# Differential-attention logits as pairs of 64-row products in the two row halves of the TensorE array

## The chip, the cores and the metric

One core of a Trainium2 chip runs the whole program. The metric is the device time of one execution in microseconds (us), median of several runs. TensorE does the matmuls, VectorE and ScalarE the elementwise work, GpSimd a few memsets and loads, and SyncE's queue issues nearly all DMAs.

## What is computed

A trunk of two layers over 512 tokens of 1024 channels. Each layer has two SwiGLU blocks, a mixer and a gated per-layer embedding; the mixer of the first layer is attention, with a sparse group of 8 heads (top-k selected keys) beside a differential group of 4 heads. The change is in the differential group. Each of its heads has two maps of 64 channels, a softmax for each, and the difference of the two acts on values of 128 channels:

```python
def diff_attention(q, k, v, lam, subln_g, lam_init):
    """q, k (B,S,H,2,HD) with the two maps on axis 3; v (B,S,H,2HD)."""
    ...
        mask = key_chunk[None, :] <= q_chunk[:, None]
        s = jnp.einsum('bqhcd,bshcd->cbhqs', qb, k).astype(jnp.float32) * scale
        prob = jax.nn.softmax(jnp.where(mask, s, -jnp.inf), axis=-1)
        a = (prob[0] - lam * prob[1]).astype(v.dtype)
        return jnp.einsum('bhqs,bshe->bqhe', a, v)
```

Queries come in blocks of 128, and block t sees the first 128(t+1) keys.

## The kernel before

**Tiling.** Activations lie transposed, channels on the 128 partitions and the 512 tokens along the free axis. `SLOTS` fixes how many buffers of each kind there are: 28 of kind "a" (128x512, floats), 12 of kind "t", 8 PSUM tiles "ps" of 128x512. A large projection is a series of `mm3` (L278 to L284): three matmuls on values split in two parts (L281, L282, L283). A plain fp32 product is `mm` (L268 to L276); in the trace each of them is two instructions on TensorE, and each instruction has its own weight load (engine PEld).

**Order of the work.** No order is written out by hand. Each helper call appends an operation with a price in ns to `Plan`; `order()` (L140) then simulates the engines and always places the operation that can start first, the lower `prio` (place in the program plus a bias for its stream) where several can. What comes out is the fixed order of each engine's queue. The price of a plain product is in `mm`, L273: 1.68 ns a column, and L274 and L275 double it for operands of at most 64 partitions; no plain product of the kernel has such operands. Operations belong to streams, and `CAPS` (L1233) limits what a stream may hold: the logits of the differential group, stream "lgpvB", may hold 2 PSUM tiles and 6 "t" tiles at a time.

**The differential group.** `even_mixer` (L773) projects queries and keys of the 4 heads into 8 tiles `bqk`, each with the two maps of a head one above the other on the partitions (64 rows each). For the keys (L936 to L945) `halves()` (L828) takes two tiles of kind "a" and sets the half that is not the map's own to zero on GpSimd; the normalised key tile is then copied half by half into them by DMA (L944). So each map has a key tile of 128 rows, half of them zero, and the product of the full query tile with it is the map's logits. `softmax_exp_` (L953) does, for each map in turn, the product (L960) and VectorE's pass that adds the mask and takes the maximum (L962); then ScalarE's exponentials (L968) with their sums. The loop of stream "pvB" (L988 to L1013) goes over 4 heads and 4 query blocks: logits, the difference of the maps, transposes, and the product with the values `bv`. `softmax_exp_` also serves the sparse group (L1034), with keys stacked to 128 rows.

**Around it.** In the same stretch TensorE has the projections for the sparse group's queries (stream "aq", L974), the embedding products (`ple_proj`, L972) and, behind the group's last head, the output projection `down` (L1027). VectorE has the 48 rounds of the top-k selection (L904 to L917) at low priority.

Of the kernel before, what the change touches and what calls it, by code (L numbers as in the profile page):

```python
# [45 lines left out]
class View:  # L46
# [19 lines left out]
    def ap(self):  # L66
        x = self.store.real
        for name, args in self.steps:
            x = getattr(x, name)(*args)
        return x  # L70
# [187 lines left out]
def trunk(ctx: ExitStack, tc: tile.TileContext, A: dict, out: bass.AP):  # L258
# [9 lines left out]
    def mm(p, a, b, start, stop):  # L268
        n = b.n
        if a.store.dt == F32R:  # L270
            cost = max(213.0 if n < 256 and n < 192 else 0.0, n * 0.422)
        else:
            cost = 150.0 if a.n <= 64 and n <= 128 else max(n, 127) * 1.68  # L273
            if a.arr.shape[0] <= 64:  # L274
                cost *= 2  # L275
        P.op("PE", cost, lambda: nc.tensor.matmul(ap(p), ap(a), ap(b), start=start, stop=stop), w=[p], r=[a, b], lat=160.0)  # L276

    def mm3(p, a, b, first, last):  # L278
# [32 lines left out]
    def dve(o, fn, r, per=1.04, extra=(), fixed=0.0):  # L311
        P.op("DVE", per * o.n + 67.0 + fixed, fn, w=[o] + list(extra), r=r)

    def tmul(o, a, b):
        dve(o, lambda: nc.vector.tensor_mul(ap(o), ap(a), ap(b)), [a, b])  # L315
# [7 lines left out]
    def ts(o, a, s1, s2, op0, op1=None):  # L323
        kw = {} if op1 is None else {"op1": op1}
        dve(o, lambda: nc.vector.tensor_scalar(ap(o), ap(a), ap(s1), ap(s2), op0=op0, **kw), [a, s1, s2],
            per=1.04 if a.psum else 0.52, fixed=62.0 * (isinstance(s1, View) or isinstance(s2, View)))

    def stt(o, a, s, b, op0, op1, accum=None):
        kw = (lambda: {"accum_out": ap(accum)}) if accum is not None else dict
        dve(o, lambda: nc.vector.scalar_tensor_tensor(ap(o), ap(a), ap(s), ap(b), op0=op0, op1=op1, **kw()), [a, s, b],  # L330
            extra=[accum] if accum is not None else [], fixed=62.0 * isinstance(s, View))
# [4 lines left out]
    def recip(o, a):  # L336
        dve(o, lambda: nc.vector.reciprocal(ap(o), ap(a)), [a], per=6.3)
# [4 lines left out]
    def gset(o, x):  # L342
        P.op("POOL", 200.0 + 0.5 * o.n, lambda: nc.gpsimd.memset(ap(o), x), w=[o])

    def dma(o, x, kb, after=None):
        P.op("SP", max(500.0, kb * 2.7), lambda: nc.sync.dma_start(ap(o), ap(x)), w=[o], r=[x, after],
             lat=2000.0 if isinstance(x, View) and isinstance(o, View) else 2000.0)
# [4 lines left out]
    def ps(shape=(128, S)):  # L352
        return P.tile("ps", shape)
# [4 lines left out]
    def at(dt=F32, shape=(128, S)):  # L358
        return P.tile("a", shape, dt)

    def tt(dt=F32, shape=(128, S)):
        return P.tile("t", shape, dt)

    def small(*n):
        return P.tile("s", (128,) + n)
# [88 lines left out]
    for part in (GAINS[:1], GAINS[1:]):  # L454
# [7 lines left out]
        with P.on("norm", 60 * (len(gcol) - 1)):  # L462
            p = ps()
# [309 lines left out]
    def even_mixer(norm, nxt, cos, sin):  # L773
# [30 lines left out]
        def head_factor(c, R):  # L804
            v, f = small(NT, R), small(NT, R)
            for t in range(NT):
                ts(v[:, t, :], c[:, t, :], rc2[:, t:t + 1], EPS, OP.mult, OP.add)
            r = rsqrt(v.flat(), NT * R)
            for t in range(NT):
                ts(f[:, t, :], r[:, R * t:R * t + R], rcol[:, t, :], None, OP.mult)  # L810
            return f
# [13 lines left out]
                        dma(d[c][0].bitcast(F32)[half, :], (hi, lo)[b].bitcast(F32)[own, :], 128)  # L825
            return d

        def halves():  # L828
            d = [at(), at()]
            gset(d[0][64:128, :], 0.0)  # L830
            gset(d[1][0:64, :], 0.0)
            return d

        wv = w.rearrange("(k p) c -> p k c", p=128)

        def values(grp):
# [22 lines left out]
        with P.on("side", SIDE_BIAS):  # L859
# [12 lines left out]
            for t in range(NT):  # L872
                p = ps()
# [11 lines left out]
        with P.on("sc", SC_BIAS):  # L885

            score = [None]
            for t in range(1, NT):
                N = 128 * (t + 1)
                sc = at()  # L890
                for h in range(4):
                    p = ps()
# [11 lines left out]
        with P.on("topk", TOPK_BIAS):  # L904

            selb = [cmask[:, S - 128:S]]
            for t in range(1, NT):
                N = 128 * (t + 1)
# [13 lines left out]
        bqk = []  # L922
        for g in range(2):
            for j in range(2):
                u = wunit(w, 0, KD, 1028 + 512 * g + 256 * j, 256)
                for s in range(2):
                    i = 4 * g + 2 * j + s
                    p = ps()
# [5 lines left out]
        with P.on("side", SIDE_BIAS):  # L934
            fB = head_factor(rows, 16)
            fq = small(NT, 8)  # L936
            ts(fq, fB[:, :, 0:8], 0.125, None, OP.mult)
            bk = []
            for h in range(4):
                fb = bcast2(fB, 8 + 2 * h)  # L940
                d = halves()
                tmul(bqk[4 + h], fb, bqk[4 + h])
                for b in range(2):
                    dma(d[b][64 * b:64 * b + 64, :], bqk[4 + h][64 * b:64 * b + 64, :], 128)  # L944
                bk.append(d)  # L945

        P.stream = "main"

        def softmax_exp(*a):
            with P.on("lg" + P.stream, LG_BIAS if P.stream == "pvB" else LGA_BIAS):  # L950
                return softmax_exp_(*a)

        def softmax_exp_(maps, N, bias, fcol):  # L953
            n = len(maps)
            mx, nb, sm = small(n), small(n), small(n)
            es = []
            for i, (q, ks) in enumerate(maps):
                p = ps()
                for j, k in enumerate(ks):
                    mm(p[:, 0:k.n], q, k, j == 0, j == len(ks) - 1)  # L960
                e = tt()
                dve(e[:, 0:N], lambda e=e, p=p, i=i: nc.vector.tensor_tensor_reduce(  # L962
                    out=ap(e[:, 0:N]), in0=ap(p[:, 0:N]), in1=ap(bias), scale=1.0, scalar=LOW,
                    op0=OP.add, op1=OP.max, accum_out=ap(mx[:, i:i + 1])), [p, bias], extra=[mx])
                es.append(e)
            stt(nb, mx, -1.0, fcol, OP.mult, OP.mult)
            for i, e in enumerate(es):
                act(e[:, 0:N], e[:, 0:N], AF.Exp, scale=fcol[:, i:i + 1], bias=nb[:, i:i + 1], accum=sm[:, i:i + 1])  # L968
            recip(sm, sm)
            return es, sm  # L970
# [3 lines left out]
        with P.on("aq", AQ_BIAS):  # L974
# [3 lines left out]
            for j in range(2):  # L978
                u = wunit(w, 0, KD, 256 * j, 256)
                for s in range(2):  # L980
                    i = 2 * j + s
                    p = ps()
# [5 lines left out]
        with P.on("pvB"):  # L988
            c = ps((128, NT, 4))
            oc = []  # L990
            for h in range(4):
                po = ps()
                for t in range(NT):
                    N = 128 * (t + 1)
                    (e0, e1), rs = softmax_exp([(bqk[h][:, 128 * t:128 * t + 128], (bk[h][c][:, 0:N],)) for c in range(2)],
                                               N, cmask[:, S - N:S], fq[:, t, 2 * h:2 * h + 2])
                    tmul(rs[:, 1:2], rs[:, 1:2], nlam)
                    scaled(e1[:, 0:N], e1[:, 0:N], rs[:, 1:2])
                    stt(e0[:, 0:N], e0[:, 0:N], rs[:, 0:1], e1[:, 0:N], OP.mult, OP.add)
                    pT = ps()  # L1000
                    for b in range(t + 1):
                        transpose(pT[:, 128 * b:128 * b + 128], e0[:, 128 * b:128 * b + 128], ident)
                    aT = tt()
                    moved(aT[:, 0:N], pT[:, 0:N])
                    for b in range(t + 1):
                        mm(po[:, 128 * t:128 * t + 128], bv[b][:, 128 * h:128 * h + 128],
                           aT[:, 128 * b:128 * b + 128], b == 0, b == t)
                o = at()
                ts(o, po, 2.0 ** 80, -2.0 ** 80, OP.min, OP.max)
                sq = tt()  # L1010
                act(sq, o, AF.Square, scale=2.0 ** -30)
                colsums(c[:, :, h:h + 1], sq, ones[:, 0:1])
                oc.append(o)  # L1013
            v, ok, fo = small(NT, 4), small(NT, 4), small(NT, 4)
            ts(ok, c, 2.0 ** 68, None, OP.is_lt)
            ts(v, c, 2.0 ** 68 * (1.0 - 2.0 ** -24), 2.0 ** 53, OP.min, OP.mult)
            ts(v, v, EPS, None, OP.add)
            r = rsqrt(v.flat(), NT * 4, 2.0 ** -40)
            tmul(fo.flat(), r, ok.flat())
            bcats = []  # L1020
            for h in range(4):
                fb = bcast(fo[:, :, h:h + 1])
                stt(oc[h], oc[h], vcol[:, 8:9], fb, OP.mult, OP.mult)
                bcats.append(split(oc[h], at))
# [5 lines left out]
        for t in range(NT):  # L1030
            N = 128 * (t + 1)
            pa = ps()
            for h in range(0, 8, 2):
                es, rs = softmax_exp([(aq[h + c][:, 128 * t:128 * t + 128], [k[:, 0:max(N, 256)] for k in ak]) for c in range(2)],  # L1034
                                     N, selb[t], fA[:, t, h:h + 2])
# [15 lines left out]
    def bcast2(f, c0):  # L1051
        p = ps()
        w = tt(shape=(128, NT, 2, 64))
        vcopy(w, f[:, :, c0:c0 + 2][:, :, :, None].to_broadcast([128, NT, 2, 64]))
        for t in range(NT):
            transpose(p[:, 128 * t:128 * t + 128], w[:, t, :, :].flat(), ident)
        return p
# [133 lines left out]
    for k in range(KD):  # L1191
        with P.on("start"):
            p = ps()
# [76 lines left out]
```

## Time and profile before

| | |
|---|---|
| median of 3 runs | 2010.78 us (2010.63 to 2011.23) |
| profiled execution | 2010.54 us |
| its span, first to last instruction | 2008.6 us |
| TensorE busy | 1991.3 us (99%) |
| weight loads busy | 1630.2 us (81%) |
| VectorE busy | 1080.8 us (54%) |
| ScalarE busy | 723.2 us (36%) |
| logits of the differential group | 490.7 to 538 us |

In the profile PE is TensorE's matmuls, PEld its weight loads, DVE VectorE, ACT ScalarE, POOL GpSimd, SPq SyncE's queue. A matmul's duration holds the time that it takes to flow through the array, so what one costs in a row of many is read from the distance of the starts. A matmul that could follow at once may be recorded as starting while the one ahead still runs.

### The profile page before, as it was taken

How to read it: one execution, taken by the hardware profiler on the slowest of the kernel's cores; microseconds unless marked ns; L12 is line 12 of the kernel's file. 1: busy time of each engine (PE TensorE's matmuls, PEld its weight loads, DVE VectorE, ACT ScalarE, POOL GpSimd, SP SyncE). 2: the span in 40 equal slices, each digit the busy share in tenths (PEclk: the TensorE clock that was granted, in tenths of full speed). 3: DMA queues.
4: the chain of work that ended last, by engine and by line, in shares of the span. 5: the costliest groups of instructions: out<-in, count | busy, mean ns of one | idle time of the engine just before them, and what ended most of it. 6: DMA issues, size and time to landing. Idle time of an engine off the chain costs nothing.

```text
span 2008.6 us, 22735 instructions
## 1 busy us (share of the span) xinstructions
PE 1991.3 (99%) x9154; PEld 1630.2 (81%) x9154; DVE 1080.8 (54%) x1797; ACT 723.2 (36%) x1057; POOL 13.8 (1%) x35
## 2 busy tenths in 40 slices
PE   8999999999999999999999999999999999999999
PEld 7888888888767888888888888888767888888887
DVE  6442464489986544344466443444699744334443
ACT  6322233344756422132254222223425533213232
POOL 0000000000000000000000000000000000000000
PEclk9999999999999999999999999999999999999999
DMA  5323322354330323332233322323333232323222
GB/s 189 105 97 98 108 85 84 94 160 141 96 110 22 104 86 105 94 95 95 95 121 110 105 98 92 105 75 103 107 105 105 84 97 92 105 85 104 95 104 75
DMA packets 164778, 202.28 MB, mean 101 GB/s; under 512 B 9968, under 2 KB 123072, under 8 KB 164672
## 3 DMA queue, kind: packets, MB, share of 16 engines
q1 hardware_dynamic: 164016, 200.38, 31.3%
q8 instruction: 72, 1.18, 0.2%
q0 software_dynamic: 528, 0.41, 0.2%
q14 instruction: 34, 0.28, 0.0%
q10 hardware_dynamic: 128, 0.03, 0.0%
HBM read 185.33 MB, written 6.29 MB: 95 GB/s over the span
## 4 chain that ended last, share of the span: by engine, by line
PE 97%; DVE 1%; ACT 1%; DMA 1%; issue 0%; SPq 0%; ACTq 0%; DVEq 0%
PE ps L281 30%; PE ps L282 30%; PE ps L283 30%; PE ps L276 6%; PE ps L287 1%; DMA whi<-in_x_dram 0%; ACT t L292 0%; ACT t L297 0%; DVE t L962 0%; DVE t L330 0%; DVE wlo L330 0%; DMA t<-t 0%; DVE t L309 0%; DVE wlo L321 0%; DVE a L913 0%
## 5 line engine op out<-in xcount | busy, mean ns | idle before, releaser
L297 ACT CAST whi<-raw 128x1024 fp32r<-128x1024 f32 (+2 forms) x342 | 348.7, 1022 | 976.3 <-PE ps L282 936.7
L321 DVE TENSOR_TENSOR wlo<-raw,whi 128x1024 fp32r<-128x1024 f32 (+2 forms) x342 | 405.1, 1185 | 496.8 <-ACT whi L297 496.0
L281 PE MATMUL ps<-x,whi 128*128 128x512 f32 x1664 | 655.8, 394 | 0.6 <-ACT x L297 0.6
L282 PE MATMUL ps<-x,whi 128*128 128x512 f32 x1664 | 648.7, 390 | 0.6 <-DVE x L321 0.6
L283 PE MATMUL ps<-x,wlo 128*128 128x512 f32 x1664 | 648.8, 390 | 0.0
L281 PEld LDWEIGHTS ps<-x,whi 128*128 128x128 f32 x1664 | 313.1, 188 | 66.2 <-ACT x L297 1.1
L283 PEld LDWEIGHTS ps<-x,wlo 128*128 128x128 f32 x1664 | 312.9, 188 | 65.6
L282 PEld LDWEIGHTS ps<-x,whi 128*128 128x128 f32 x1664 | 313.2, 188 | 65.1 <-DVE x L321 1.2
L281 PE MATMUL ps<-a,whi 128*128 128x512 f32 x832 | 325.1, 391 | 0.0
L282 PE MATMUL ps<-a,whi 128*128 128x512 f32 x832 | 323.9, 389 | 0.0
L283 PE MATMUL ps<-a,wlo 128*128 128x512 f32 x832 | 323.8, 389 | 0.0
L281 PEld LDWEIGHTS ps<-a,whi 128*128 128x128 f32 x832 | 156.3, 188 | 32.8 <-issue 0.5
L283 PEld LDWEIGHTS ps<-a,wlo 128*128 128x128 f32 x832 | 156.2, 188 | 32.6
L282 PEld LDWEIGHTS ps<-a,whi 128*128 128x128 f32 x832 | 156.2, 188 | 32.3 <-DVE a L321 0.7
L315 DVE TENSOR_TENSOR t<-ps,t 128x512 f32<-128x512 f32 x88 | 60.8, 691 | 209.1 <-PE ps L283 208.3
L315 DVE TENSOR_TENSOR t<-ps,rb 128x512 f32<-128x512 f32 x100 | 68.7, 687 | 112.1 <-PE ps L283 109.9
L330 DVE SCALAR_TENSOR_TENSOR a<-a 128x508 f32<-128x508 f32 (+23 forms) x108 | 72.7, 731 | 5.0 <-ACT a L292 4.6
L292 ACT ACTIVATE t<-t 128x512 f32<-128x512 f32 x100 | 62.9, 629 | 22.9 <-DVE t L315 22.8
L297 ACT CAST a<-t 128x512 fp32r<-128x512 f32 x88 | 54.8, 623 | 36.8 <-DVE t L315 36.8
L315 DVE TENSOR_TENSOR t<-t,rb 128x512 f32<-128x512 f32 x92 | 63.2, 687 | 1.2
L321 DVE TENSOR_TENSOR a<-t,a 128x512 fp32r<-128x512 f32 x88 | 60.4, 686 | 5.2 <-ACT a L297 4.8
L276 PE MATMUL ps<-a 128*128 128x512 f32 (+3 forms) x152 | 58.6, 501 | 1.5 <-ACT t L297 0.5
(167 smaller groups left out, 1358.8 us busy)
## 6 DMA issues: line engine op xcount, KB each, us to landing
raw<-in_ffn_wg_dram SPq DMA_DIRECT2D x43, 1024.0 KB, 5.1
raw<-in_ffn_wu_dram SPq DMA_DIRECT2D x43, 1024.0 KB, 5.1
raw<-in_ffn_wd_dram SPq DMA_DIRECT2D x40, 1024.0 KB, 4.9
raw<-in_ple_wgate_dram SPq DMA_DIRECT2D x8, 1024.0 KB, 5.0
raw<-in_od_w_in_dram SPq DMA_DIRECT2D x8, 1024.0 KB, 5.5
raw<-in_ev_w_in_dram SPq DMA_DIRECT2D x7, 1024.0 KB, 5.8
raw<-in_ffn_wd_dram SPq DMA_DIRECT2D x8, 512.0 KB, 3.7
raw<-in_ev_w_out_dram SPq DMA_DIRECT2D x4, 1024.0 KB, 5.3
```

Source lines behind the costliest of these rows:

```text
L276: P.op("PE", cost, lambda: nc.tensor.matmul(ap(p), ap(a), ap(b), start=start, stop=stop), w=[p], r=[a, b], lat=160.0)
L281: nc.tensor.matmul(q, x, u, start=first, stop=False)
L282: nc.tensor.matmul(q, x, v, start=False, stop=False)
L283: return nc.tensor.matmul(q, y, u, start=False, stop=last)
L287: P.op("PE", 107.0, lambda: nc.tensor.transpose(ap(p), ap(x), ap(idn)), w=[p], r=[x, idn], lat=160.0)
L292: P.op("ACT", cost, lambda: nc.scalar.activation(ap(o), ap(x), func, scale=ap(scale), bias=ap(bias), **({"accum_out": ap(accum)} if accum ...
L297: P.op("ACT", 0.83 * o.n + (52.0 if x.psum else 93.0), lambda: nc.scalar.copy(ap(o), ap(x)), w=[o], r=[x])
L315: dve(o, lambda: nc.vector.tensor_mul(ap(o), ap(a), ap(b)), [a, b])
L321: dve(o, lambda: nc.vector.tensor_sub(ap(o), ap(a), ap(b)), [a, b])
L330: dve(o, lambda: nc.vector.scalar_tensor_tensor(ap(o), ap(a), ap(s), ap(b), op0=op0, op1=op1, **kw()), [a, s, b], extra=[accum] if accum i ...
```

## The change

The two tiles for each head's keys, their memsets and the copies go away: the two maps' keys are the two row halves of the normalised key tile itself, and the query of a map is the same half of the query tile. So each logits product has operands of 64 partitions, 0 to 63 for the first map and 64 to 127 for the second. In `softmax_exp_` the PSUM tiles of both maps are made first and both products are issued ahead of VectorE's passes; this holds for the sparse group too. The planner's price of a product of at most 64 rows becomes half the usual one plus 45 ns.

```diff
@@ mm
             cost = 150.0 if a.n <= 64 and n <= 128 else max(n, 127) * 1.68
             if a.arr.shape[0] <= 64:
-                cost *= 2
+
+                cost = cost / 2 + 45.0
@@ even_mixer
-        def halves():
-            d = [at(), at()]
-            gset(d[0][64:128, :], 0.0)
-            gset(d[1][0:64, :], 0.0)
-            return d
-
...
             for h in range(4):
                 fb = bcast2(fB, 8 + 2 * h)
-                d = halves()
                 tmul(bqk[4 + h], fb, bqk[4 + h])
-                for b in range(2):
-                    dma(d[b][64 * b:64 * b + 64, :], bqk[4 + h][64 * b:64 * b + 64, :], 128)
-                bk.append(d)
+                bk.append([bqk[4 + h][64 * b:64 * b + 64, :] for b in range(2)])
@@ softmax_exp_
-            for i, (q, ks) in enumerate(maps):
-                p = ps()
+            logits = [ps() for _ in maps]
+            for p, (q, ks) in zip(logits, maps):
                 for j, k in enumerate(ks):
                     mm(p[:, 0:k.n], q, k, j == 0, j == len(ks) - 1)
+            for i, p in enumerate(logits):
                 e = tt()
@@ even_mixer, stream "pvB"
-                    (e0, e1), rs = softmax_exp([(bqk[h][:, 128 * t:128 * t + 128], (bk[h][c][:, 0:N],)) for c in range(2)],
+                    (e0, e1), rs = softmax_exp([(bqk[h][64 * c:64 * c + 64, 128 * t:128 * t + 128], (bk[h][c][:, 0:N],)) for c in range(2)],
```

## Rows read from the trace of the kernel before

**Rows 1.** Page, part 4: the chain that ended last, shares by engine

```profile
PE 97%; DVE 1%; ACT 1%; DMA 1%; issue 0%; SPq 0%; ACTq 0%; DVEq 0%
```

**Rows 2.** Busy time by window: start:end, length, PE, PEld, DVE, ACT, POOL, PEclk, DMA, GB/s

```profile
480.00:538.00 58.00, 56.65 (x315) 44.23 (x313) 56.44 (x196) 38.66 (x94) 0.52 (x1) 1.00 0.44 124
...
592.00:629.00 37.00, 32.56 (x247) 24.93 (x245) 26.82 (x100) 28.18 (x75) 0.00 (x0) 1.00 0.12 37
```

**Rows 3.** Timeline of PE (start, us, what, count), logits pairs back to back, what follows

```profile
496.05 1.88 PE L276 MATMUL ps<-a 128*128 128x512 f32 x4
497.77 0.27 PE L287 MATMUL ps<-ident,t 128*128 128x128 f32 x1
...
504.05 1.56 PE L276 MATMUL ps<-a 128*128 128x384 f32 x4 [0.47 <-DVE s L962]
505.44 0.83 PE L276 MATMUL ps<-t,a 128*128 128x128 f32 x6
...
514.24 1.02 PE L276 MATMUL ps<-a 128*128 128x256 f32 x4
515.10 0.38 PE L276 MATMUL ps<-t,a 128*128 128x128 f32 x2
```

**Rows 4.** Timeline of PE, logits pairs with other work between their two products

```profile
498.58 0.38 PE L276 MATMUL ps<-a 128*128 128x128 f32 x2
...
499.50 0.38 PE L276 MATMUL ps<-a 128*128 128x128 f32 x2
499.72 0.39 PE L276 MATMUL ps<-t,a 128*128 128x128 f32 x2
...
506.43 1.02 PE L276 MATMUL ps<-a 128*128 128x512 f32 x2
...
509.22 1.02 PE L276 MATMUL ps<-a 128*128 128x512 f32 x2
```

**Rows 5.** Timeline of PE, the sparse group's products in column halves (128*64)

```profile
574.53 0.43 PE L276 MATMUL ps<-t,a 128*64 128x128 f32 x2
574.89 0.39 PE L276 MATMUL ps<-a,x 128*128 128x256 f32 x1
...
575.92 0.40 PE L283 MATMUL ps<-a,wlo 128*128 128x512 f32 x1
576.25 0.44 PE L276 MATMUL ps<-t,a 128*64 128x128 f32 x4
576.61 0.50 PE L281 MATMUL ps<-a,whi 128*128 128x512 f32 x1
576.95 0.40 PE L282 MATMUL ps<-a,whi 128*128 128x512 f32 x1
```

**Rows 6.** Timeline of PE, a transpose of 48 rows among projection matmuls

```profile
18.05 0.39 PE L283 MATMUL ps<-x,wlo 128*128 128x512 f32 x1
18.37 0.26 PE L287 MATMUL ps<-ident,t 48*128 48x48 f32 x1
18.56 0.50 PE L281 MATMUL ps<-x,whi 128*128 128x512 f32 x1
18.90 0.39 PE L282 MATMUL ps<-x,whi 128*128 128x512 f32 x1
```

**Rows 7.** Timeline of PE, a transpose of 128 rows among projection matmuls

```profile
571.85 0.39 PE L283 MATMUL ps<-a,wlo 128*128 128x512 f32 x1
572.08 0.27 PE L287 MATMUL ps<-ident,t 128*128 128x128 f32 x1
572.10 0.47 PE L281 MATMUL ps<-a,whi 128*128 128x512 f32 x1
572.42 0.39 PE L282 MATMUL ps<-a,whi 128*128 128x512 f32 x1
```

**Rows 8.** Timeline, all engines: copies of the key halves, last memset for them

```profile
487.47 4.35 SPq L346 DMA_DIRECT2D a<-a  x7
...
490.82 0.52 POOL L343 MEMSET a<- 64x512 f32 x1 [57.44 <-DMA a<-a]
```

## The prediction

> **What bounds the kernel now.** Read the chain of work that ended last first: it is TensorE almost from end to end [rows 1], so a product that is taken out or made dearer counts unless TensorE was waiting there. Then the busy time by stretch. The logits of the differential attention stand between 490.7 and 538 us; there TensorE and VectorE are both taken (56.65 and 56.44 of 58 us), because the 48 rounds of the top-k selection fill VectorE wherever the softmax leaves it free; the granted clock is 1.00, the upper level, throughout [rows 2]. Neither engine has much slack there, so what TensorE gains or loses shifts the stretch. After 592 us the second half of the attention ends the mixer with TensorE idle for 4.4 of 37 us [rows 2]; that idle time, a turn-taking of three engines, is not touched.
>
> **The products, now.** One fp32 product is two matmul instructions, each with its own weight load. A group of four is the pair of maps back to back: with 512 columns it starts at 496.05 and the next instruction at 497.77, so 0.43 us an instruction; with 256, 514.24 to 515.10, 0.215; with 384, 504.05 to 505.44, 1.39 us, of which 0.10 is a first weight load that no earlier matmul hid, so 0.32; with 128, two in 0.22 us, 0.11 each [rows 3, 4]. Call these T. A pair takes 4T: 0.44, 0.86, 1.29 and 1.72 us, and four heads 17.2 us. The zero rows are paid in full.
>
> **What the change saves at best.** If the two halves of the array work at the same time, a pair takes 2T: 8.6 us less over 16 pairs. No row shows row halves side by side. The nearest are the products of the other attention, in column halves: two instructions of one half last from 574.53 to the next start at 574.89, 0.36 us; four, two for each half, from 576.25 to 576.61, the same 0.36 us [rows 5]. So halves do overlap, also when one half's two instructions stand ahead of the other's. I take full overlap; the other end is none.
>
> **What it adds: leaving and re-entering the whole array.** Around those column products the stream stands still. From 575.92 (a 512-column matmul) over the four to the second matmul behind them at 576.95 it is 1.03 us; whole-array work would be 0.23 + 0.22 + 0.23 = 0.68 [rows 5]. An excursion costs 0.35 us: about 0.10 before it, 0.05 for a half-width weight load that nothing hides, and the rest at the exit, where the following weight load isn't hidden either. Does it hold for rows? A transpose of 48 rows, the row case nearest to 64, sits between two dense matmuls: from 18.05 to the second matmul behind it is 0.85 us [rows 6], against 0.57 for the same neighbours around a full transpose [rows 7]. So 0.28 us more, though this transpose is smaller. For rows the weights are 128 columns wide, and an unhidden load of those is the 0.10 us above, not 0.05: 0.40 us an excursion. I take 0.40, with 0.28 as the low end. Where TensorE had waited before the product anyway, the first half (0.20) is already paid.
>
> The Trainium skill, "TensorEngine Tiling (Array Packing)", Key Properties, says that changing the tiling mode, not just the tile, drains the engine; the trace agrees, with the 0.10 us that pass between the stream and the 48-row transpose. The section speaks against a change that makes short visits to the half mode among whole-array work.
>
> **How many excursions.** The list planner gives an engine whatever can start first, and a stream of these logits may hold two PSUM buffers. The second map's buffer comes free only after VectorE's later pass of the pair before, so often a filler is put between the two products. I followed the groups through the timeline: of the 16 pairs 8 stand back to back (one with 128 columns, two with 256, two with 384, three with 512), as in rows 3, and 8 are parted by a projection triple, a transpose or a PV product, as in rows 4. The change sets both PSUM tiles up ahead of the loop and issues the products before the VectorE passes in program order, but buffers and limit stay, and a planner that thinks the first product shorter (153 to 475 ns instead of 215 to 860) leaves the second less time to become ready. I keep 8 and 8; the ends are 4 and 16.
>
> - The 8 together: 2T each, 0.22 + 2 x 0.43 + 2 x 0.645 + 3 x 0.86 = 4.95 us saved; 8 x 0.40 = 3.2 us added, less 2 x 0.2 for the two 384-column pairs where TensorE had waited. Net 2.15 us saved.
> - The 8 parted: each product runs alone in its half, takes its 2T as before, and makes an excursion of its own: 16 x 0.40 = 6.4 us, less 0.4 where one adjoins the next pair in the half mode, less 0.3 for two with the wait already there. Net 5.7 us added.
>
> Together TensorE gets **3.6 us more** work, in a stretch where it is the bound.
>
> **The rest.** Eight memsets of 0.52 us on GpSimd go; it stood idle for 57.4 us ahead of the last one, nobody waited: nothing [rows 8]. Eight key copies go from SyncE's queue, 7 in 4.35 us from 487.47 [rows 8]; behind them in that queue stand the rotary swaps of the next projection, which leave up to 4.4 us earlier. The first logits can start up to some 3 us earlier (the copies' issue at 487.47 against 490.67), but TensorE had projections to do meanwhile; nothing, with the low end at 3 us gained if the fillers run out instead. The copied keys' buffers shrink by four of 28; no wait for one is on the path. VectorE's work is the same. What could hurt is the plan: it prices the logits at 10.0 us in all, they would take 20.8, so VectorE's passes are queued for earlier times, each in order ahead of top-k rounds that could have run. Who waits for these is the last top-k selection. Since both engines shift together I count 0 for it, with 5 us as the upper end.
>
> **The rivals.**
> - *All pairs stay together*, since the program order now has them adjacent: 8.6 us saved, 16 x 0.40 - 0.4 = 6.0 added, so 2.6 us faster: 2008.2. For it: half already are. Against: the second buffer decides. Chance 0.20.
> - *Faster: pairs together and cheap switches.* If row halves switch without the exit cost, some 0.1 us an excursion, and all pairs are together, 8.6 - 1.6 = 7.0 us go: 2003.8. It decides from an excursion below 0.28 us, the row of the 48-row transpose, so that row speaks against it. Chance 0.12. The Trainium skill, "TensorE: Matmul & The Clock Gate", Part 3, gives this result: packed tiles take one product's time and about 4 ns for each further tile. The trace agrees on the overlap (four column products in the time of two) but not on what stands around it.
> - *Slower still: hardly any pair together, or VectorE held up by the plan.* With 4 together, 4 x (0.54 - 0.40) saved and 24 x 0.40 added is 9.0 us: 2019.8; 5 us of VectorE stalls on the forecast gives the same. Chance 0.20.
> - *It doesn't do what it says*: the halves take turns. Then nothing is saved, and 8 + 16 excursions less the shared and waited ones cost 2.8 + 5.7 = 8.5 us: 2019.3. Rows 5 speak against it, for columns. Chance 0.08.
>
> **How the numbers follow.** The sum is made against the profiled execution, 2010.54 us (span 2008.6 and 1.9 around it), which lies 0.24 below the median of 2010.78. 2010.54 + 3.6 = 2014.1, about 2014.3 on the median's scale. This has chance 0.40, and alone reaches from 2011 to 2017 (excursions of 0.28 to 0.45 us, 6 to 10 pairs together). 0.2% is 4.0 us, about what a measurement of this kernel can tell from no change. Of the forecast 0.25 lies within that and 0.15 above; of the first rival 0.18 within and 0.02 below; the faster rival lies below, the last two above. So faster 0.14, same 0.43, slower 0.43. The range from 2006 to 2020 leaves out the faster rival and the worst of the slow ones.
>
> **What the new profile would show.** The overlap is right if a pair that stands together has its third and fourth instructions start beside the first two, and four of 512 columns take about 0.9 us instead of 1.72. The price is right if 0.09 to 0.1 us more than usual stands ahead of each 64-row product and the matmul behind the exit needs 0.34 instead of 0.23. The count is right if the timeline has some 8 groups of four and some 16 of two. VectorE's waits for the logits' PSUM between 490 and 545 us should leave it idle some 1.6 us of 58, as now; if that grows by several us, the plan's price was the cause. The prediction is wrong if the pairs are all together, or if a switch between row halves and the whole array is far cheaper than that between columns.

## The result, and the profile after

The changed kernel takes 2038.69 us (2038.11 to 2040.82, four runs) beside 2010.7 us for the kernel before (2010.54 to 2011.23, four runs): **1.4% slower**, ratio 1.0141 with a 95% interval of 1.0123 to 1.0158. That is 28 us more, where 3.6 were forecast and 2020 us was the top of the range. The profiled execution of after takes 2038.81 us, with a span of 2037.0.

Nothing in the page's shares gives the reason away. TensorE is as full as before and the chain is still its own (PE 98%, [rows 1]). The first sign stands in the row of granted clocks: one of forty slices, the eleventh, stands at 7 instead of 9. These are lines of parts 1, 2 and 4 of the page of after.

```profile
PE 2012.9 (99%) x9154; PEld 1637.6 (80%) x9154; DVE 1084.6 (53%) x1801; ACT 725.9 (36%) x1055; POOL 9.5 (0%) x27
...
PEclk9999999999799999999999999999999999999999
...
PE 98%; DVE 1%; ACT 0%; DMA 0%; issue 0%; SPq 0%; DVEq 0%; ACTq 0%
```

The windows find the place (columns as in rows 2). The attention of the first layer ends where TensorE starts the last output projection, at 628.84 us before and at 655.66 after, so 26.8 of the 28 us arise ahead of it. First that start and the whole stretch from 480 us, before and then after:

```profile
628.84 0.50 PE L281 MATMUL ps<-x,whi 128*128 128x512 f32 x1 [0.35 <-ACT x L297]
...
480.00:628.80 148.80, 143.05 (x829) 107.95 (x827) 132.08 (x440) 99.14 (x241) 0.52 (x1) 1.00 0.33 96
```

```profile
655.66 0.50 PE L282 MATMUL ps<-x,whi 128*128 128x512 f32 x1 [0.36 <-ACT x L298]
...
480.00:655.70 175.70, 162.93 (x835) 114.40 (x833) 135.93 (x445) 100.81 (x240) 0.00 (x0) 0.92 0.25 76
...
480.00:538.40 58.40, 56.31 (x276) 37.33 (x274) 48.43 (x158) 33.42 (x78) 0.00 (x0) 1.00 0.39 113
538.40:558.90 20.50, 17.34 (x56) 12.48 (x56) 14.92 (x53) 10.04 (x22) 0.00 (x0) 0.50 0.33 90
```

The number of instructions is nearly the same (829 and 835), yet three things differ. TensorE is busy 19.9 us longer. It stands idle for 12.8 us instead of 5.75 (length less busy time). And from 538.4 to 558.9 it runs at a granted clock of 0.50, the level of 1.2 GHz; with two shorter stretches at 620.4 and 640.8 us that makes 27.3 us at the lower level, of which the kernel before has none here (1.00). In the first 58 us VectorE also works 8 us less than in the nearly equal stretch of [rows 2]. The timeline of TensorE in after, with one of its weight loads, shows what came ahead of the fall:

```profile
534.33 1.92 PE L277 MATMUL ps<-a 64*128 64x512 f32 x4 [0.42 <-DVE s L955]
535.13 0.29 PEld L277 LDWEIGHTS ps<-a 64*128 64x128 f32 x2 [0.51 <-DVE s L955]
536.94 0.49 PE L277 MATMUL ps<-a 64*128 64x128 f32 x2 [0.69 <-DVE s L955]
540.94 1.11 PE L288 MATMUL ps<-ident,t 128*128 128x128 f32 x4 [3.52 <-ACT t L293]
```

The engine stood for 0.42, 0.69 and then 3.52 us, and 1 us into the last wait the clock fell. So TensorE, which the forecast took for always fed in this stretch, ran out of work. VectorE did too. Its waits between 490 and 545 us, the longest groups of before and of after (waited for: us in all, times, longest), make 1.1 us of waiting before and 9.3 us after:

```profile
DVE t L330 <- DMA t<-t: 0.6, 1, 0.6
DVE a L315 <- PE ps L287: 0.3, 1, 0.3
DVE t L962 <- PE ps L287: 0.2, 1, 0.2
```

```profile
DVE s L338 <- ACT t L293: 2.8, 1, 2.8
DVE t L955 <- PE ps L277: 2.2, 4, 0.9
DVE t L310 <- PE ps L288: 1.9, 3, 1.2
DVE t L955 <- PE ps L288: 1.8, 2, 1.2
```

**An account of the 26.8 us**, from these rows: products in half the array 7.4 us (25 excursions, that is visits to half the array, of 0.40, less 2.6 saved by five pairs that run side by side; both are read below), the lower clock at most 27.3 / 2 = 13.65, further idle time of TensorE 7.0. That is 28.05, some 1.2 too much, since TensorE stands still for 3.2 us of the stretch at the lower clock and half of that is counted twice. A sixth pair, the one of 512 columns at 534.33, stands together too, but the weights of its second product are loaded only at 535.13, behind a wait on VectorE; it lasts 1.92 us, no less than in the whole array (1.72), and is counted as saving nothing. The account says where the time lies, not what caused it. For that the change is taken apart.

### The profile page after: what moved, and what is told of

Same layout as the page of the kernel before. It is cut to its first block, busy times and chain, and to the rows that moved or that the text cites. A ratio compares the mean times of both kernels' runs of the same rounds, so it can differ in the third digit from the quotient of the medians.

```text
span 2037.0 us, 22700 instructions
## 1 busy us (share of the span) xinstructions
PE 2012.9 (99%) x9154; PEld 1637.6 (80%) x9154; DVE 1084.6 (53%) x1801; ACT 725.9 (36%) x1055; POOL 9.5 (0%) x27
## 4 chain that ended last, share of the span: by engine, by line
PE 98%; DVE 1%; ACT 0%; DMA 0%; issue 0%; SPq 0%; DVEq 0%; ACTq 0%
PE ps L282 30%; PE ps L283 30%; PE ps L284 30%; PE ps L277 7%; PE ps L288 2%; DMA whi<-in_x_dram 0%; DVE wlo L331 0%; ACT t L293 0%; DVE t L955 0%; DVE t L310 0%; DVE h L319 0%; DVE wlo L322 0%; DVE t L331 0%; ACT x L298 0%; DVE x L322 0%
## 5 line engine op out<-in xcount | busy, mean ns | idle before, releaser
L282 PE MATMUL ps<-x,whi 128*128 128x512 f32 x1664 | 655.7, 394 | 0.6 <-ACT x L298 0.6
L277 PE MATMUL ps<-a 128*128 128x512 f32 (+6 forms) x152 | 63.6, 549 | 2.0 <-DVE s L955 1.3
```

The costliest lines, as they stand in the source:

```text
L282: nc.tensor.matmul(q, x, u, start=first, stop=False)
```

## The experiments

### Plan and products, one at a time

The change does two things: it gives the planner other prices and buffers, so that another order comes out, and it sends the logits through half the array. Each was tried alone.

**The products alone.** The kernel before with its plan, copies and memsets; a logits product merely takes its map's 64 rows.

```diff
-            if a.arr.shape[0] <= 64:
-                cost *= 2
...
-softmax_exp([(bqk[h][:, 128 * t:128 * t + 128], (bk[h][c][:, 0:N],)) for c in range(2)],
+softmax_exp([(bqk[h][64 * c:64 * c + 64, 128 * t:128 * t + 128], (bk[h][c][64 * c:64 * c + 64, 0:N],)) for c in range(2)],
```

> The kernel before, its plan, memsets, copies and queue orders unchanged; only each logits product works on its own 64 rows of the same tiles. Theory P (the plan's wrong price makes the 28 us, the products themselves cost little): 8 pairs together save 2.2 us, 8 parted ones add 5.7 us, so about +3.6 us, 2012 to 2017 us, no long idle stretch of TensorE and no half clock in the mixer. Theory H (the half-array products themselves, with what they stop, make most of it): 2030 us or more, with the half clock as in the changed kernel.

Measured: 2015.77 us beside 2011.24, ratio 1.0020 (1.0011 to 1.0029): **+4.0 us** by the ratio, where the prediction's sum for this order was +3.6. The traces of this kernel and of before have the instructions of each engine, by operation and tiles, in the same order. Up to the end of the attention, 4.8 us later than before, the clock stayed at 1.00:

```profile
480.00:633.60 153.60, 148.28 (x840) 105.63 (x839) 133.72 (x444) 100.77 (x242) 0.52 (x1) 1.00 0.31 93
```

**The plan alone.** The changed kernel with its own plan, but each logits product on all 128 rows.

```diff
...
+        x, y = (whole(a), whole(b)) if a.arr.shape[0] <= 64 else (a, b)
...
```

Here `whole` (not shown) turns a slice of 64 rows into all 128 rows of the same tile, and the matmul takes `x` and `y`.

> The changed kernel with its plan and queue orders, but each logits product runs on all 128 rows of the key and query tiles, so the zero halves are missing and each product is the sum of both maps (that part of the result differs). No half-array products are left. Theory P: the queues are still ordered for products of half the time, TensorE still falls behind the plan and VectorE and TensorE still wait for each other: 2022 us or more. Theory H: without half-array work the time is back within 4 us of the kernel before, 2007 to 2015 us.

Measured: 2028.81 us, 1.0087 (1.0072 to 1.0102): **+17.5 us** without a single product in half the array. Its trace has the instructions of each engine in the order of after. Its timeline has the same waits, the long one included, and the windows have 17.1 us at the lower clock (13.7 from 535.7, 3.4 from 631.3):

```profile
531.28 0.49 PE L285 MATMUL ps<-a 128*128 128x128 f32 x2 [0.63 <-DVE s L963]
535.28 0.72 PE L296 MATMUL ps<-ident,t 128*128 128x128 f32 x4 [3.51 <-ACT t L301]
...
480.00:646.20 166.20, 153.52 (x834) 116.11 (x832) 135.26 (x444) 100.33 (x240) 0.00 (x0) 0.95 0.26 80
...
535.70:549.40 13.70, 13.08 (x49) 10.89 (x47) 10.05 (x38) 8.62 (x19) 0.00 (x0) 0.50 0.36 107
```

So the order that came out costs most of the 28 us, and the half-array products did not make the long wait.

**The usual price in the changed kernel**, with 64 and with 128 rows. The rule for narrow operands goes, so the planner again sees 1.68 ns a column; the second kernel takes all 128 rows as above.

```diff
-            if a.arr.shape[0] <= 64:
-                cost = cost / 2 + 45.0
```

> The changed kernel, but the planner takes a logits product for as long as a full one (1.68 ns a column). Memsets, copies and zero tiles are gone as in the change. Theory P: planned times are near the real ones (one alone takes 0.40 us more than planned, a pair together less), so 2010 to 2017 us. Theory H: 2030 us or more, since the same half-array products run.

> The run with the old price again, same plan and queue orders, but each logits product on all 128 rows of key and query tile (so each is the sum of both maps; that part of the result differs). Theory X (excursions: 26 of them at 0.40 us less the 3 us that five pairs together saved, plus one short half clock, make that run's 10 us): 2010 to 2014 us. Theory L (that run's plan is an unlucky one, whatever the products are): 2017 us or more.

Measured: 2020.87 us, 1.0051 (1.0036 to 1.0066), +10.3 us, and 2013.88 us, 1.0011 (1.0001 to 1.0020), +2.2 us. The first lies between its two theories, the second within the first of its own. On this third order too the half-array products cost, some 8 us. Both kernels also do without the memsets and copies; no gain from that shows, though with a third order it isn't measured by itself.

**The pair as one operation of the plan**, so that its two products can't be parted, at its true price (the planner was extended to give one operation two buffers).

```diff
-            for p, (q, ks) in zip(logits, maps):
-                for j, k in enumerate(ks):
-                    mm(p[:, 0:k.n], q, k, j == 0, j == len(ks) - 1)
...
+                def both():
+                    for p, q, k in prods:
+                        last = nc.tensor.matmul(ap(p), ap(q), ap(k), start=True, stop=True)
+                    return last
+                P.op("PE", max(N, 127) * 1.68 + 400.0, both, w=[x[0] for x in prods], r=[v for x in prods for v in x[1:]], lat=160.0)
...
```

> The changed kernel, but the two products of a pair are one operation of the plan, so all 16 pairs stand together, at a price of one full product plus 400 ns. TensorE should have 8.6 us less of products and 16 excursions of 0.40 us, 2.2 us less in all. Theory P: 2005 to 2012 us, no long idle stretch. Theory H (half-array work itself stops the stream): 2020 us or more.

Measured: 2017.87 us, 1.0031 (1.0019 to 1.0044), **+6.2 us**. That again lies between the two theories. All 16 pairs stand together (in one of them the second product still waits), so the products should give some 2.2 us back (8.6 saved, 16 x 0.40 added); it is slower all the same, and the profiled execution, 2021.40 us, has 17.1 us at the lower clock and 2.2 us more idle time. One of the stretches at the lower clock began at 514.1 us, where TensorE had not been waiting: its busy time there is the whole window.

```profile
512.38 0.49 PE L952 MATMUL ps<-a 64*128 64x128 f32 x4
512.80 1.05 PE L274 MATMUL ps<-ones,t 128*128 128x1 f32 x8
...
512.00:516.00 4.00, 4.00 (x22) 2.37 (x21) 3.96 (x16) 2.74 (x8) 0.00 (x0) 0.76 0.20 56
```

### Is it that the price is wrong?

The prediction had named the price: the planner thinks the logits take 10.0 us and they take 20.8. If that were the cause, a truthful price would mend it, and the kernel before, whose price is nearly truthful, should mind an untrue one. Five kernels before, untouched but for the price of these 32 products (half and 45 ns; 400 ns more; 10 ns less; 5 and 45 ns more), and the changed kernel with 400 ns more:

```diff
-            if a.arr.shape[0] <= 64:
-                cost *= 2
+            if P.stream == "lgpvB":
+                cost = cost / 2 + 45.0
```

In the others the price in the last line is `cost + 400.0`, `cost + -10.0`, `cost + 5.0` and `cost + 45.0`; in the changed kernel the rule for narrow operands becomes `cost + 400.0`.

> The kernel before with its zero tiles, copies and full products, only the planner's price of a logits product is the changed one (half plus 45 ns). Theory W (the wrong price spoils the plan: it prices 17.2 us of products at 10.0): 2018 us or more, TensorE idle several us between 480 us and the mixer's end, a half clock there. Theory C (what spoiled the changed plan is the missing copies or the new loop order): 2008 to 2014 us.

> The changed kernel, but the planner takes a logits product for a full one plus 400 ns, what one alone really takes. Theory X: the number of excursions decides; with some 24 to 26 of them 2016 to 2020 us, like the run with the old price. Theory W (the planned times decide even where they are off by 0.4 us a product): clearly below that run, 2014 us or less.

> The kernel before with its full products; only the planner's price of a logits product is 400 ns dearer than it is. Theory W (only a price too low harms, since TensorE then runs behind its plan): 2009 to 2014 us. Rival (any other plan costs, since this one is a good draw): 2016 us or more.

> The kernel before, its work unchanged; the planner's price of a logits product is 10 ns lower (32 products, 0.3 us in all). Theory D (the order before is a good draw, and any change of the planner's numbers draws another): 2015 us or more. Theory W (only a price that is far off harms): 2008 to 2014 us.

> The kernel before, its work unchanged; the planner's price of a logits product is 5 ns higher (0.2 us in all). Theory D: anything from 2010 to 2025 us, as likely above 2014 as below. Theory W: 2008 to 2014 us.

> The kernel before, its work unchanged; the planner's price of a logits product is 45 ns higher (1.4 us in all). Theory D: 2015 us or more. Theory W: 2008 to 2014 us.

| kernel | price of the logits | median, us | ratio (95%) | difference by the ratio, us |
|---|---|---|---|---|
| changed | true, + 400 ns | 2026.77 | 1.0082 (1.0066 to 1.0097) | +16.5 |
| before | too low, half + 45 ns | 2021.50 | 1.0053 (1.0036 to 1.0069) | +10.7 |
| before | too high, + 400 ns | 2023.62 | 1.0052 (1.0039 to 1.0066) | +10.5 |
| before | - 10 ns | 2022.99 | 1.0055 (1.0034 to 1.0076) | +11.1 |
| before | + 5 ns | 2014.19 | 1.0012 (1.0003 to 1.0021) | +2.4 |
| before | + 45 ns | 2022.24 | 1.0046 (1.0031 to 1.0061) | +9.3 |

As the one cause the theory falls. A price that is too low and one that is too high cost nearly the same, 10.7 and 10.5 us, and so does one that is off by 10 ns, 1 to 5% of a product's price and far below any error in it. The true price mends the changed kernel by some 12 us of 28 only, and leaves it above both theories of its run. What the six have in common is that the order is another one: in the traces 211 (5 ns more) to 561 (400 ns more) of TensorE's 9154 instructions stand at another place in its queue than before. With 10 ns less, the stretch from 480 us reads

```profile
480.00:642.50 162.50, 153.10 (x835) 115.73 (x833) 136.87 (x447) 97.52 (x236) 0.52 (x1) 0.95 0.30 88
```

that is 9.4 us idle, 17 us at the lower clock, and the same work as before. So **the order of the kernel before is a good draw of its planner** (a draw: one of the many orders that come out for nearly the same input): of the orders tried without any change of the products (these five of before, and the two of the changed kernel with 128 rows) none is faster, two cost some 2 us, four 9 to 11, one 17.5. Whether that is luck isn't shown; the biases and limits of the planner may have been chosen with this order. Nor is it shown that the low price has no part in it: the changed plan, the worst of the seven, has it.

### Filling the wait

Does the long wait cause the rest, by the fall of the clock behind it? In the changed kernel thrown-away products were put in TensorE's queue where it would stand still: ahead of the transposes at 540.94, then, in a second kernel, one product earlier (`fill` does the matmul in the comment).

```diff
...
+            due = halves == 25 and o.eng == "PE" and not o.half and fill is not None
+            if due:
+                for _ in range(4):
+                    fill(target)    # matmul(p[:, 0:512], ident, cmask)
...
+            due = halves == 25 and o.half and fill is not None
+            if due:
+                for _ in range(5):
+                    fill(target)    # matmul(p[:, 128:512], ident, cmask[:, 0:384])
...
```

> The changed kernel with its plan; only four full-array fp32 products of 512 columns, whose result is thrown away, stand in TensorE's queue where it waits 3.5 us ahead of the half clock (3.4 us of work at the full clock). Theory K (the clock falls because TensorE stands still there, and the 20 us at half clock cost about 10 us): the half clock of 20 us is gone, 2026 to 2032 us. Theory A (half-array products keep the clock down by themselves, wait or no wait): half clock at the same place, 2036 us or more.

> The changed kernel with its plan; five full-array fp32 products of 384 columns, thrown away, stand ahead of the logits product behind which TensorE waits 3.5 us (3.2 us of work at the full clock, written beside that product's columns in its own PSUM tile). Theory K (standing still starts the half clock, and its 20 us cost about 10): no half clock from 538 us on, 2026 to 2032 us. Theory A (the clock falls whatever TensorE does there): half clock near 538 us as before, 2036 us or more.

Measured: 2042.98 us, 1.0154 (1.0131 to 1.0177), and 2039.45 us, 1.0135 (1.0118 to 1.0151). In the first kernel the added products themselves waited for their PSUM tile, for 3.60 us, so that run decides nothing:

```profile
541.71 5.40 PE L1232 MATMUL ps<-cmask,ident 128*128 128x512 f32 x8 [3.60 <-ACT t L302]
```

In the second they ran for 3.46 us ahead of the wait, and the clock held there. But a wait of 1.14 us came behind them, the clock fell at 549.5 for 17.1 us, and one more of 1.20 us followed:

```profile
540.93 3.46 PE L1232 MATMUL ps<-cmask,ident 128*128 128x384 f32 x10 [0.78 <-DVE s L964]
549.38 1.89 PE L285 MATMUL ps<-a 64*128 64x256 f32 x4 [1.14 <-DVE s L964]
552.47 0.80 PE L285 MATMUL ps<-a,x 128*128 128x256 f32 x2 [1.20 <-DVE s L964]
...
540.00:549.50 9.50, 7.18 (x37) 4.96 (x37) 9.39 (x27) 5.97 (x13) 0.00 (x0) 1.00 0.59 168
549.50:566.60 17.10, 15.28 (x43) 9.33 (x43) 8.97 (x34) 8.33 (x19) 0.00 (x0) 0.50 0.06 15
```

What it expected if the one wait were the whole cause, 2026 to 2032 us, did not come: the shortage of work moved to the next place. TensorE waits for VectorE there, which is busy for 9.39 of those 9.50 us.

### A version that keeps the order

If order is what counts, the half-array products must be had without a new draw. The kernel before with 64-row products has its pairs brought together in the finished order, each first product moved down to its second.

```diff
...
+    halves = [o for o in P.ops if o.half]
+    for one, two in zip(halves[::2], halves[1::2]):
+        i, j = order.index(one), order.index(two)
...
+            for o in order[i + 1:j]:
+                if o.deps & moved_:
+                    moved_.add(o)
+                    later.append(o)
+                else:
+                    kept_.append(o)
+            order[i:j + 1] = kept_ + [one, two] + later
...
```

> The run with the plan of before and 64-row products, but in the finished order the first product of each parted pair stands right ahead of the second, and what needs it behind. All 16 pairs together, 16 excursions in place of 23: 8.6 us of products less, 16 x 0.40 = 6.4 us more, less 0.7 where TensorE waits anyway. Theory X (excursions decide): 2.9 us faster than the kernel before, so 2007 to 2010 us on its scale of 2011. Rival (TensorE's gain is eaten by VectorE's later passes, by waits or half clocks): 2012 us or more.

Measured: 2011.9 us beside 2011.5, ratio 0.9997 (0.9988 to 1.0006): **no difference from before that can be measured**, and some 4 us better than with the pairs parted. All 16 pairs are together and the clock stays at 1.00 up to the end of the attention; of the 2.9 us hoped for, 1.4 went into idle time (7.15 us up to 631.2 where before has 5.75), and some 1.5 into four pairs whose second product was held up and that last longer than the others of their size (1.38 us instead of 0.92 at 506.54, for one). The whole stretch, and one of the waits:

```profile
480.00:631.20 151.20, 144.05 (x847) 104.73 (x845) 134.21 (x445) 100.31 (x242) 0.52 (x1) 1.00 0.31 95
...
497.83 1.13 PE L274 MATMUL ps<-a 64*128 64x512 f32 x4
500.18 0.33 PE L286 MATMUL ps<-ident,t 128*128 128x128 f32 x1 [1.22 <-DVE t L329]
```

Fewer visits still, with the pairs of a head's first two query blocks as one operation, side by side in the same two PSUM tiles (12 visits in all):

```diff
...
+                    if t != 1:
+                        done = logits_of(h, (0, 1) if t == 0 else (t,))
...
```

> The run with the pair as one operation, and the first two query blocks of a head together too, their logits side by side in the same two PSUM tiles: 12 excursions in place of 16. Theory X: TensorE has 8.6 us less of products and 12 x 0.40 = 4.8 us of excursions, 3.8 us less in all: 2006 to 2010 us if its waits stay as in the kernel before; 2012 to 2017 us if the waits and half clocks of the run with 16 come back.

Measured: 2031.34 us, 1.0105 (1.0090 to 1.0120), +21 us: a new draw once more, in which the group's output projection fell behind the sparse group. No version here beats the kernel before.

## Why the prediction was wrong

**The account over all the orders.** The time at which the attention ends, and what the windows from 480 us to it say, in the one profiled execution of each kernel:

| kernel | products | end, us | later than before | idle, us | at lower clock, us |
|---|---|---|---|---|---|
| before | 128 rows | 628.8 | | 5.75 | 0 |
| its order | 64 rows | 633.6 | 4.8 | 5.3 | 0 |
| its order, pairs brought together | 64 rows | 631.2 | 2.4 | 7.15 | 0 |
| changed, usual price | 128 rows | 633.1 | 4.3 | 5.55 | 3.4 |
| changed, usual price | 64 rows | 638.7 | 9.9 | 5.2 | 3.4 |
| changed, pair as one | 64 rows | 638.3 | 9.5 | 8.0 | 17.1 |
| changed, true price | 64 rows | 644.7 | 15.9 | 9.75 | 13.7 |
| changed | 128 rows | 646.2 | 17.4 | 12.7 | 17.1 |
| changed | 64 rows | 655.7 | 26.8 | 12.8 | 27.3 |
| before, 10 ns less | 128 rows | 642.5 | 13.7 | 9.4 | 17.1 |
| before, + 5 ns | 128 rows | 632.2 | 3.4 | 5.75 | 3.4 |
| before, + 45 ns | 128 rows | 639.2 | 10.4 | 7.55 | 13.7 |
| before, half + 45 ns | 128 rows | 640.0 | 11.2 | 10.45 | 10.2 |
| before, + 400 ns | 128 rows | 642.9 | 14.1 | 14.75 | 10.2 |

For each row the products' price, half the time at the lower clock and the further idle time sum to the delay within 3 us (3.2 where the pairs were brought together; TensorE has done 18 more instructions there by 631.2 than before by 628.8, so some later work is in it). Take the changed plan with 128 rows: 0 + 8.55 + 6.9 = 15.5 of 17.4. With the pair as one: -2.2 + 8.55 + 2.2 = 8.6 of 9.5.

The part of the clock can be read apart from the order. Executions of one kernel have the same order and the same products, and still differ in the mean granted clock: the pair as one operation took 2015.33 us at a mean of 0.998 and 2021.40 at 0.994, the kernel with 10 ns less 2018.78 at 0.997 and 2027.82 at 0.993. A mean that is lower by 0.004 is 8 us of 2020, and the times are 6.1 and 9.0 us apart. Likewise 0.999 before and 0.992 after make some 14 of the 28 us. Their idle time isn't on record. So far as that goes, the cost of the lower clock is borne out with the order held, and an order alone doesn't settle how long the clock stays low.

**Right: the halves overlap.** The rival that they take turns is out. In after a pair of 384 columns lasts from 531.89 to the next start at 532.74, 0.85 us, and a single product of 384 columns from 495.11 to 495.95, 0.84; with the order of before, a pair of 512 takes 1.06 us and in after a single product 1.05. In the whole array such a pair took 1.29 and 1.72 [rows 3]. This holds where the second product can start; of the eight pairs that stand together in the order of before, two had it held up and saved less (with 64 rows a pair of 384 columns at 506.86 lasts 1.63 us, one of 128 at 526.40 0.85), which the prediction did not count. The timeline of after, and then of before's order with 64 rows:

```profile
495.11 0.91 PE L277 MATMUL ps<-a 64*128 64x384 f32 x2
495.95 0.50 PE L282 MATMUL ps<-x,whi 128*128 128x512 f32 x1
...
498.93 0.39 PE L284 MATMUL ps<-x,wlo 128*128 128x512 f32 x1
499.25 1.12 PE L277 MATMUL ps<-a 64*128 64x512 f32 x2
500.30 0.50 PE L282 MATMUL ps<-x,whi 128*128 128x512 f32 x1
500.64 0.39 PE L283 MATMUL ps<-x,whi 128*128 128x512 f32 x1
...
531.89 0.92 PE L277 MATMUL ps<-a 64*128 64x384 f32 x4
532.74 0.94 PE L277 MATMUL ps<-t,a 128*128 128x128 f32 x6
```

```profile
498.55 1.13 PE L274 MATMUL ps<-a 64*128 64x512 f32 x4
499.61 0.33 PE L285 MATMUL ps<-ident,t 128*128 128x128 f32 x1
```

The Trainium skill, "TensorE: Matmul & The Clock Gate", Part 3, gives a pack the time of one product and some ns; the 0.01 us between these pairs and single products agree with it.

**Right: the price of an excursion.** From 498.93 (a projection matmul) over the single 512-column product to the second matmul behind it, at 500.64, is 1.71 us; whole-array work would be 0.23 + 0.86 + 0.23 = 1.32. That is 0.39 us, taken at 0.40 from column halves and the 48-row transpose [rows 5, 6]. The parts are those that the prediction named: 0.32 instead of 0.23 ahead of the product, 0.34 instead of 0.23 for the matmul behind it. That a change of mode drains the engine, the rule of "TensorEngine Tiling (Array Packing)" in the Trainium skill (Key Properties), was rightly weighed against the change. The rival with cheap switches is out.

**Nearly right: the count.** After has 25 excursions with 6 pairs together, where 8 together were counted and some 23; in this order the products are worth up to +7.4 us by the same prices instead of +3.6. On the order that the count was made from, the sum held: +4.0 measured.

**Wrong: "I count 0 for it, with 5 us as the upper end"**, the sentence on the plan. The order that came out costs 17.5 us by itself, and it is the term that put the time outside the range. Two things were missed. The step argued that both engines shift together; instead each came to wait for the other, TensorE for 7.0 us more up to the end of the attention and VectorE for 8.2 us more in the 55 us from 490. And it priced a wait at its own length. In this kernel a shortage of work costs more: in all the orders of the table with more than 7.5 us of idle time the lower clock came with it, 10 to 27 us long, and half of that is lost again (in the others it is none or 3.4 us). The prediction read the clock at 1.00 [rows 2] and did not consider that it could fall.

**The reason given for the risk was wrong too.** The last part said that if VectorE's waits grew by several us the plan's price was the cause. They grew, but a wrong price isn't needed for the loss, as 10 ns of change and a true price show; with the true price VectorE waits for only 0.4 us between 490 and 545 us, and the kernel still loses 16.5. What the runs show in its place is that a planner which places by "who can start first" gave another order for every other price tried, down to 5 ns, and the one of before is the best of those tried. The rival "VectorE held up by the plan" was the right kind, a loss by the plan, with 5 us in place of what measured 17.5.

**Smaller terms.** Memsets and copies were put at nothing, and no gain from them shows in any run, though none has them alone. Of the 28 us, 26.8 are gone at the end of the attention; a further 1.7 is one stretch at the lower clock near 1590 us, which lasts 3.4 us longer than the one that the kernel before has near 1565 (half of 3.4).

**What stays open.** No run took the waits away and left the rest: filling one wait moved both idle time and lower clock. And the fall at 514 us with the pair as one operation had no long wait ahead of it. So that the waits bring the clock down is what the timelines suggest, not what a run has shown. How the remaining 10.5 us between the changed plan with 128 and with 64 rows divide is worked out only (up to 7.4 for products, 5.1 for more time at the lower clock, together 2 too much), not measured apart; the same products cost 4.0 us in the order of before.

## What to carry to other kernels

Where a list planner writes the order, a change is a new draw before it is anything else: run the old operations in the new order and the new operations in the old order, and change a price by a few ns to see how wide the draws scatter (here 2 to 11 us, where the change with all pairs together could gain 2.2 by the measured prices). Price a new order not at zero but by that scatter, and ask of each wait on an engine that has always been fed what its clock will do behind it. Packing two of these 64-row fp32 products pays only where they stand together, both can start at once, and they are long: a visit to half the array costs 0.40 us, which a pair of 128 columns (0.22 saved) does not earn back and one of 512 (0.86) does.

## What the runs showed of the hardware

Four things about the granted clock were not expected. It fell to 0.50 behind waits far shorter than the 3.5 us one: in the second kernel with added products 0.1 us behind a wait of 1.14 us, in a stretch where TensorE had been idle for 2.3 of 9.5 us; and once, at 514.1 us with the pair as one operation, with no wait in the two us ahead of it, only 64-row products, sums of one column, a transpose and a few projections. It stayed at 0.50 while TensorE was busy again, for 13.08 of 13.70 us with the changed plan and 128 rows. And in the first kernel with added products it came back at 545.2 us, while these dense products ran (541.71 to 546.95), and fell again at 555.4. And between executions of one kernel, with one order, the mean granted clock differs, from 0.993 to 0.997 with 10 ns less. What decides is not settled by these runs.
